# Half of an expert's down product as three float32r products, and two expert weights stored in 4 KB rows

## The chip, the cores and the metric

The kernel runs on one core of a Trainium2 chip. The metric is the device time of one execution in microseconds (us). A core has five engines that run side by side and meet through semaphores: TensorE (PE in the profile; its weight loads are listed apart as PEld), VectorE (DVE), ScalarE (ACT), GpSimd (POOL) and SyncE (SP, which here only issues transfers). Each engine works through its own instructions in program order.

## The reference

One encoder layer over 1,024 prompt tokens and 256 sample tokens of width 1,024, all in float32: a modulated RMS norm, an input projection, two token mixers (neighbourhood attention and multi-head latent attention), a gated merge, an output projection, and a mixture of experts; then a last norm. Only the mixture of experts is touched. A router gives each of the 1,280 tokens one of 4 groups and in it 2 of 8 experts, so 2,560 pairs of a token and an expert go to 32 experts. For each block of up to 128 tokens of one expert:

```
def expert_block(args):
    xb, e = args
    return (jax.nn.silu(xb @ w1[e]) * (xb @ w3[e])) @ w2[e]
```

with `w1[e]` and `w3[e]` of 1024 x 512 and `w2[e]` of 512 x 1024. The result is weighted and added to the token's row.

## The kernel before

The kernel goes through the layer in stages. The last long one is the expert stage, from about 1195 us to 1812 us: one block of 128 rows for each of the 32 experts, written out as a Python loop over `e` from 0 to 32, and after it a loop on the chip for experts with more than 128 tokens. With these inputs that loop runs zero times: the trace has 32 blocks.

A TensorE product takes a stationary operand (128 x 128) and a moving operand (128 rows, up to 512 columns). Two kinds of product occur here. A product of two float32 operands is recorded by the trace as two matrix instructions. The other kind is float32r, a reduced form, recorded as one. To keep the accuracy of float32 with it, the kernel splits a float32 array into a high part (the array rounded to float32r) and a low part (what is left), and adds up three products: high by high, low by high, high by low. `w_split` does this for a weight tile of 128 x 1024: ScalarE writes the high part (line 1399), VectorE subtracts it for the low part (line 1400).

An expert's weights come as 12 tiles of 512 KB ("quarters"): four of W1 (`m` is 0), four of W3 (`m` is 1), four of W2 (`m` is 2). `w_load` (line 1394) issues each on SyncE's queue into a free slot of 4 KB in each partition. A quarter of W1 or W3 is two blocks of 128 x 512, so that a partition receives two rows of 2 KB; a quarter of W2 is one block of 128 x 1024, one row of 4 KB. `w_ahead` issues the next loads of the fixed order `stream` as soon as slots are free, so loads run far ahead of use. Splits run three quarters ahead: when quarter i is taken (`w_next`), `w_fill` puts the split of quarter i + 3 into the programs of ScalarE and VectorE. The parts lie in a ring of 8 slots, four pairs, so the split of quarter i + 3 waits until TensorE is done with quarter i - 1.

The order of the work in a pass of the loop over `e`, the same on every engine:

- `up(0)` for expert e (line 1540): 24 float32r products, 4 quarters of 6; then ScalarE's silu (line 1545)
- `aT` for expert e - 1: 4 transposes of the activations on TensorE (line 1553), a copy of the 128 x 512 result by ScalarE (line 1555)
- `up(1)` for expert e: again 24 products; then VectorE's product with the silu (line 1547)
- `xT` for expert e + 1: 8 transposes of its gathered rows (line 1527), split by ScalarE (line 1529) and VectorE (line 1530); its rows come from `gather` (line 1370), issued by GpSimd
- `down` for expert e - 1: first the row `y` of gains (lines 1560 and 1561), then for each of 4 quarters of W2 two float32 products, one for each half of the 1,024 columns (line 1566), then VectorE's two scalings (line 1571), and GpSimd's scatter that adds the rows to `x1_d` (line 1572)

`xH`, `xL` and `y` take their slots from a ring of three.

Of the kernel before, what the change touches and what calls it, by code (L numbers as in the profile page):

```python
# [10 lines left out]
F32 = mybir.dt.float32  # L11
F32R = mybir.dt.float32r
# [74 lines left out]
def f32(x):  # L87
    return x.bitcast(F32)


def v3(t, k):
    return t.rearrange("p (k n) -> p k n", k=k)
# [3 lines left out]
def kernel(ctx, tc, A, out_p, out_s, upto=99, dbg=None):  # L96
    nc = tc.nc
    ctx.enter_context(tc.manual_schedule())
    V, S, G, PE, SY = nc.vector, nc.scalar, nc.gpsimd, nc.tensor, nc.sync
# [974 lines left out]
    n = len(units)  # L1074
# [307 lines left out]

    W1, W3, W2 = [A[n][0] for n in ("expert_w1", "expert_w3", "expert_w2")]
    stream = [(e - (m == 2), m, q) for e in range(33) for m in range(3) for q in range(4) if 0 <= e - (m == 2) and (e < 32 or m == 2)]
    LEAD, ACTS = 3, 3

    def w_load(e, m, q):
        r = sl.get()  # L1390
        src = (W1, W3, W2)[m]
        src = src[e] if isinstance(e, int) else src[bass.ds(e, 1)].rearrange("o r n -> (o r) n")
        k = 2 if m < 2 else 1
        SY.dma_start(v3(r, k), src.rearrange("(k p) n -> p k n", p=128)[:, q * k:q * k + k, :])
        return r

    def w_split(r):
        hi, lo = sl.get(F32R, parts), sl.get(F32R, parts)
        S.copy(hi, r)  # L1399
        V.tensor_sub(lo, r, f32(hi))  # L1400
        sl.put(r)
        w_ahead(0)
        return hi, lo

    loaded, ready = {}, deque()
    halves = [k for k in stream if k[1] < 2]
    at = [0, 0, 0]

    def w_ahead(spare):
# [4 lines left out]

    def w_next(e, m, q):

        if m == 2:
            return loaded.pop((e, m, q))
        assert halves[at[2]] == (e, m, q)
        at[2] += 1  # L1420
        w_fill()
        return ready.popleft()
# [90 lines left out]
    class Block:  # L1513
# [36 lines left out]
        def aT(b):  # L1550
            p = psx.tile([128, 4, 128], F32, name="pt")
            for k in range(4):
                PE.transpose(p[:, k, :], b.a[:, k * 128:k * 128 + 128], ident)  # L1553
            b.aT_ = ep.tile([128, 4, 128], F32, name="aT")
            S.copy(b.aT_, p)  # L1555

        def down(b, quarter):

            y = sl.get(ring=acts)
            S.mul(y, g2[1], b.of[1])  # L1560
            V.scalar_tensor_tensor(y, g2[0], b.of[0], y, op0=OP.mult, op1=OP.add)
            ps = [psh.tile([128, 512], F32, name=f"py{hb}") for hb in range(2)]
            for k in range(4):
                w = quarter(2, k)
                for hb, p in enumerate(ps):
                    PE.matmul(p, b.aT_[:, k, :], w[:, hb * 512:hb * 512 + 512], start=(k == 0), stop=(k == 3))  # L1566
                sl.put(w)
                w_ahead(0)
            for hb, p in enumerate(ps):
                cs = slice(hb * 512, hb * 512 + 512)  # L1570
                V.scalar_tensor_tensor(y[:, cs], p, b.wcol, y[:, cs], op0=OP.mult, op1=OP.mult)  # L1571
            G.indirect_dma_start(out=x1_d, out_offset=bass.IndirectOffsetOnAxis(ap=b.ix, axis=0), in_=y,  # L1572
                                 in_offset=None, bounds_check=NTOK - 1, oob_is_err=False, compute_op=OP.add)
            sl.put(y)
# [50 lines left out]
    with tc.For_i(0, n_rv, 1):  # L1625
        pick = ep.tile([128, 4], F32, name="pick")
        V.tensor_scalar(c, left, -BIG, BIG, op0=OP.mult, op1=OP.add)
        V.tensor_add(c, c, io9)
        V.tensor_reduce(pick[:, 0:1], c, axis=AX.XY, op=OP.min)
        V.tensor_scalar(c, c, pick[:, 0:1], None, op0=OP.is_equal)  # L1630
        V.tensor_sub(left, left, c)
        for k in range(2):
            V.tensor_mul(c2[:, k], be[:, k], c)
            V.tensor_reduce(pick[:, 1 + k:2 + k], c2[:, k], axis=AX.XY, op=OP.add)
        eint = ep.tile([128, 1], I32, name="eint")
        V.tensor_copy(eint, pick[:, 2:3])
        posb = ep.tile([128, 2, NT], F32, name="posb")
        V.tensor_scalar(posb, pos, pick[:, 1:2], None, op0=OP.subtract)
        eq = ep.tile([128, 2, NT], F32, name="eq")
        V.tensor_scalar(eq, eid, pick[:, 2:3], None, op0=OP.is_equal)  # L1640
        R = ep.tile([128, 2, NT, 2], F32, name="oR")
        for k in range(2):
            V.tensor_mul(R[:, k, :, 0], eq[:, k], tok1)
            V.tensor_mul(R[:, k, :, 1], eq[:, k], wgt[:, k])
        ps = psx.tile([128, 4, 128], F32, name="pt")
        for k in range(2):
            for t in range(NT):
                oh = ep.tile([128, 128], F32, name="ooh", bufs=2)
                V.tensor_scalar(oh, iof, posb[:, k, t:t + 1], None, op0=OP.is_equal)
                PE.matmul(ps[:, 0, :2], oh, R[:, k, t, :], start=(k == 0 and t == 0), stop=(k == 1 and t == NT - 1))  # L1650
        osl = ep.tile([128, 5], F32, name="osl")
        V.tensor_copy(osl[:, 0:2], ps[:, 0, :2])
        V.tensor_scalar(osl[:, 2:3], osl[:, 0:1], 0.0, 4096.0, op0=OP.is_equal, op1=OP.mult)
        ix = ep.tile([128, 1], I32, name="oix")
        V.scalar_tensor_tensor(ix, osl[:, 0:1], -1.0, osl[:, 2:3], op0=OP.add, op1=OP.add)
        for g, op in enumerate((OP.is_le, OP.is_gt)):
            V.tensor_scalar(osl[:, 3 + g:4 + g], osl[:, 0:1], float(SP), None, op0=op)
        e_rv = SY.value_load(eint[0:1, 0:1], min_val=0, max_val=31)
        b = Block(ix, osl[:, 1:2], [osl[:, 3 + g:4 + g] for g in range(2)])
        b.gather()  # L1660
        raws = {(m, q): w_load(e_rv, m, q) for m in range(3) for q in range(4)}
        b.xT()
        quarter = lambda m, q: w_split(raws[m, q]) if m < 2 else raws[m, q]
        b.up(0, quarter)
        b.up(1, quarter)
        b.aT()
        b.down(quarter)
# [37 lines left out]
def layout(inputs):  # L1705

    a = {k: np.ascontiguousarray(inputs[k]) for k in _INS}
    q = a["w_uq"].reshape(1, 256, 8, 96)
    a["w_uq"] = np.ascontiguousarray(np.concatenate(
        [q[..., :64].reshape(1, 256, 512), q[..., 64:].reshape(1, 256, 256)], axis=2))  # L1710
    kv = a["w_ukv"].reshape(1, 128, 8, 128)
    a["w_ukv"] = np.ascontiguousarray(np.concatenate(
        [kv[..., :64].reshape(1, 128, 512), kv[..., 64:].reshape(1, 128, 512)], axis=2))
    inv = (np.float32(1.0) / np.power(np.float32(10000.0), np.arange(0, 32, 2, dtype=np.float32) / np.float32(32)))
    ang = np.arange(SP, dtype=np.float32)[:, None] * inv[None, :].astype(np.float32)
    c, s = np.cos(ang).astype(np.float32).T, np.sin(ang).astype(np.float32).T
    cs = np.stack([np.tile(np.concatenate(x), (4, 1)) for x in ((c, c), (-s, s))])
    a["rope_p"] = by_blocks(cs[..., None])[..., 0]
    a["rope_s"] = np.ascontiguousarray(cs[:, :, :SS])
    a["x_prompt"] = by_blocks(a["x_prompt"])  # L1720

    rpb = a.pop("na_rpb")[0]
    row, c8, col = np.arange(16), np.arange(8), np.arange(64)
    rs = np.clip(row - 4, 0, 8)
    rows = (row[None, :] >= rs[:, None]) & (row[None, :] < rs[:, None] + 8)
    dr = np.clip(row[None, :] - row[:, None] + 7, 0, 14)
    dc = 8 * (np.arange(3)[None, :, None] - 1) + c8[None, None, :] - c8[:, None, None]
    val = rpb[:, dr[:, None, None, :, None], np.clip(dc + 15, 0, 30)[None, :, :, None, :]]  # L1730
    m0 = np.broadcast_to(rows[:, None, None, :, None], val.shape[1:]) & (np.abs(dc) < 16)[None, :, :, None, :]
    m1 = m0 & ((dc >= -8) & (dc < 8))[None, :, :, None, :]
    a["nbias"] = np.ascontiguousarray(np.stack(
        [np.where(m, val, np.float32(NEG)).reshape(8, 128, 384) for m in (m0, m1)], axis=2).reshape(8, 128, 768))
    st = np.clip(col - 8, 0, 48)
    inside = (col[None, :] >= st[:, None]) & (col[None, :] < st[:, None] + 16)
    dr = np.arange(6)[None, :] + 5 - np.arange(2)[:, None]
    dc = np.clip(col[None, :] - col[:, None] + 15, 0, 30)
    val = rpb[:, dr[:, None, :, None], dc[None, :, None, :]]
    a["sbias"] = np.ascontiguousarray(np.where(inside[None, None, :, None, :], val, np.float32(NEG)).reshape(8, 128, 384))  # L1740
    return a
# [18 lines left out]
```

## Time and profile before

| | |
|---|---|
| time before, median of 3 runs | 1855.91 us (1853.6 to 1859.47) |
| the profiled execution's own time | 1854.83 us |
| its span, first to last instruction | 1853.1 us |
| TensorE busy | 1743.1 us, 94% of the span |
| VectorE busy | 1001.4 us, 54% |
| ScalarE busy | 838.8 us, 45% |
| expert weights loaded | 384 transfers of 512 KB |

In rows of the profile `out<-in` are the names of tiles (`s` is any slot, `ph` and `pt` and `py` are PSUM tiles), a count follows an x, and an arrow `<-` behind an idle time names what ended it. A busy share of an engine is an average over stages with different limits. The ends of matrix instructions are modelled, so a busy TensorE need not be at its peak.

### The profile page before, as it was taken

Reading aid. Unit: us, or ns where it says so; the run is one execution under the profiler, and the core shown is the slowest. Engines: PE = TensorE matmul, PEld = TensorE weight load, DVE = VectorE, ACT = ScalarE, POOL = GpSimd, SP = SyncE. Lnnn points to the kernel's source line nnn. Section 1 sums busy time; section 2 is a strip of 40 time slices with the busy share of each in tenths; the row PEclk is TensorE's granted clock in tenths of the full one; section 3 lists DMA queues with packets and bytes.
Section 4 is the critical chain, followed back from the end, with each engine's and each line's share of the span. In section 5 each row is a group of like instructions: output and inputs, shape, how many; then the busy total and the mean of one; then the engine's idle time right before and its main releaser. Section 6 shows DMA issues by size and latency. Waiting matters only on the chain.

```text
span 1853.1 us, 27078 instructions
## 1 busy us (share of the span) xinstructions
PE 1743.1 (94%) x9874; PEld 1357.6 (73%) x9874; DVE 1001.4 (54%) x1674; ACT 838.8 (45%) x1391; POOL 319.0 (17%) x329
## 2 busy tenths in 40 slices
PE   5999999999999999999899999699999999999991
PEld 4787777998888888767688877567676676766760
DVE  6324422111455655444357466777777777777764
ACT  6222222321455555666533213366556565655642
POOL 0010210000122222322333000111111111111110
PEclk9989999999999999999899999799999999999995
DMA  9335676536714442878977356899999999999916
GB/s 349 109 115 168 222 264 221 191 91 165 152 55 112 115 121 86 232 214 230 297 251 224 132 216 235 327 359 360 361 365 360 362 356 361 358 356 364 349 36 242
DMA packets 268848, 439.47 MB, mean 237 GB/s; under 512 B 31928, under 2 KB 131592, under 8 KB 268712
## 3 DMA queue, kind: packets, MB, share of 16 engines
q1 hardware_dynamic: 252008, 389.45, 62.8%
q0 software_dynamic: 13824, 37.77, 7.3%
q10 hardware_dynamic: 2880, 10.49, 1.4%
q8 instruction: 79, 1.29, 0.3%
q14 instruction: 57, 0.47, 0.1%
HBM read 367.53 MB, written 82.67 MB: 243 GB/s over the span
## 4 chain that ended last, share of the span: by engine, by line
PE 84%; DVE 5%; DMA 5%; issue 2%; ACT 2%; SPq 1%; POOL 1%; DVEq 0%; POOLq 0%; ACTq 0%; another core or an unknown queue 0%
PE ph L1540 19%; PE pg L432 13%; PE py L1566 11%; PE s L895 6%; PE pw L1303 5%; PE fp L766 5%; PE fp L678 4%; PE o L945 4%; PE tp L927 4%; PE pg L599 3%; PE pt L1527 2%; PE pg L341 1%; PE pg L557 1%; PE pt L1553 1%; DMA x_d<-s,idx 1%
## 5 line engine op out<-in xcount | busy, mean ns | idle before, releaser
L1540 PE MATMUL ph<-s,s 128*128 128x512 f32 x1536 | 377.0, 401 | 1.4 <-DVE s L1530 1.2
L1399 ACT CAST s<-s 128x1024 fp32r<-128x1024 f32 x256 | 265.9, 1055 | 194.2 <-PE ph L1540 193.9
L1540 PEld LDWEIGHTS ph<-s,s 128*128 128x128 f32 x1536 | 286.4, 188 | 73.8 <-issue 13.9
L1400 DVE TENSOR_TENSOR s<-s,s 128x1024 fp32r<-128x1024 f32 x256 | 304.5, 1221 | 63.7 <-ACT s L1399 57.4
L432 PE MATMUL pg<-s,s 128*128 128x512 f32 (+1 forms) x1416 | 270.2, 351 | 7.8 <-ACT s L182 4.2
L432 PEld LDWEIGHTS pg<-s,s 128*128 128x128 f32 x1416 | 226.8, 190 | 53.0 <-ACT s L182 4.9
L1566 PE MATMUL py<-s,aT 128*128 128x512 f32 x512 | 225.1, 592 | 0.7 <-ACT aT L1555 0.7
L917 POOL TENSOR_SCALAR s<-s,m 128x1024 f32<-128x1024 f32 (+2 forms) x160 | 122.8, 767 | 438.5 <-DVE m L916 363.6
L1566 PEld LDWEIGHTS py<-s,aT 128*128 128x128 f32 x512 | 94.8, 190 | 108.2 <-issue 100.0
L895 PE MATMUL s<-s,s 96*128 96x512 f32 (+2 forms) x592 | 147.7, 368 | 1.8 <-ACT s L913 1.4
L913 ACT ACTIVATE s<-s,m 128x1024 f32<-128x1024 f32 (+2 forms) x160 | 124.9, 781 | 46.6 <-DVE m L903 27.3
L929 ACT COPY s<-tp 128x512 f32<-128x512 f32 (+2 forms) x160 | 78.2, 488 | 120.5 <-PE tp L927 116.9
L895 PEld LDWEIGHTS s<-s,s 96*128 96x128 f32 (+1 forms) x592 | 109.9, 190 | 27.9 <-ACT s L913 2.3
L678 PE MATMUL fp<-s,s 128*128 128x512 f32 x384 | 126.4, 430 | 2.8 <-ACT s L682 2.6
L927 PE MATMUL tp<-ident,s 128*128 128x128 f32 x752 | 110.4, 275 | 9.8 <-POOL s L917 9.4
L183 DVE TENSOR_TENSOR s<-s,s 128x1024 fp32r<-128x1024 f32 x31 | 37.7, 1224 | 148.7 <-ACT s L182 137.0
L1303 PE MATMUL pw<-s,s 128*128 128x512 f32 x480 | 118.0, 400 | 0.0
L766 PE MATMUL fp<-s,s 128*128 128x512 f32 (+1 forms) x576 | 114.0, 359 | 2.8 <-DMA s<-ao_m 1.4
L903 DVE TENSOR_REDUCE m<-s 128x1 f32<-128x1024 f32 (+1 forms) x80 | 85.0, 1062 | 51.6 <-PE s L895 50.2
L1572 POOL DMA_INDIRECT x_d<-s,idx x32 | 71.7, 2242 | 231.1 <-DVE s L1571 116.1
L766 PEld LDWEIGHTS fp<-s,s 128*128 128x128 f32 x576 | 96.5, 191 | 20.1 <-DMA s<-ao_m 2.1
L927 PEld LDWEIGHTS tp<-ident,s 128*128 128x128 f32 x752 | 89.3, 141 | 25.3 <-POOL s L917 15.9
(225 smaller groups left out, 2012.3 us busy)
## 6 DMA issues: line engine op xcount, KB each, us to landing
s<-in_expert_w SPq DMA_DIRECT2D x384, 512.0 KB
s<-in_w_in SPq DMA_DIRECT2D x47, 512.0 KB
s<-in_ada_w POOLq DMA_DIRECT2D x32, 512.0 KB, 6.1
s<-nak_d SPq DMA_DIRECT2D x40, 256.0 KB
s<-in_x_prompt SPq DMA_DIRECT2D x16, 512.0 KB
s<-in_ada_w SPq DMA_DIRECT2D x16, 512.0 KB
s<-gate_d SPq DMA_DIRECT2D x16, 512.0 KB
gate_d<-s SPq DMA_DIRECT2D x16, 384.0 KB
```

What stands on the lines that cost most here:

```text
L432: PE.matmul(p[:m, :CHUNKS[c][1]], g.at(a, j, 0, m), b.at(j, c), start=(j == 0 and n == 0), stop=(j == KD - 1 and n == 2))
L678: PE.matmul(p, w.at(a, j), b.at(j, 0), start=(n == 0), stop=(n == 23))
L766: PE.matmul(p[:, :w], b.ws[i].at(u, x * 4 + j), o[:, v, :w], start=(m == 0), stop=(m == 11))
L895: PE.matmul(u.s[:, b, :u.w], a, c, start=(n == 0), stop=(n == len(ops) - 1))
L913: S.activation(u.out, u.src, AF.Exp, bias=u.m[:, 0:1], scale=u.sign, accum_out=u.m[:, 1:2])
L917: G.tensor_scalar(u.P[:, :u.n], u.P[:, :u.n], u.m[:, 2:3], 1.0, op0=OP.mult, op1=OP.mult)
L927: PE.transpose(tp[:w, i // 128, :], u.P[:, b * 512 + i:b * 512 + i + w], ident)
L1303: PE.matmul(b.p, x[b.c].at(k, b.c, b.k), w[:, k % 2, :], start=(k + i == 0), stop=(k == 7 and i == 2))
L1399: S.copy(hi, r)
L1400: V.tensor_sub(lo, r, f32(hi))
L1540: PE.matmul(p, a[:, 2 * q + k, :], v3(w, 2)[:, k, :], start=(q + k + i == 0), stop=(q == 3 and k == 1 and i == 2))
L1566: PE.matmul(p, b.aT_[:, k, :], w[:, hb * 512:hb * 512 + 512], start=(k == 0), stop=(k == 3))
```

## The change

Of the four quarters of W2, the first two are now split as W1 and W3 are, and their part of the down product is done in three float32r products each; the other two stay float32. So a pass splits 10 quarters instead of 8, and the order of the splits (`halves`) takes in the two quarters of W2 behind the eight of the expert that follows. In `aT` the first two of the four transposed blocks become a high part (ScalarE) and a low part (VectorE, straight from PSUM), and ScalarE copies the other two: one copy of 128 x 512 becomes three instructions of 128 x 256. The ring of parts keeps its 8 slots. On the host, W1 and W3 are stored in a new array `w13` such that each quarter's 4 KB for a partition lie in one row; the values and the slots' contents stay the same.

```
+    W13, W2 = A["w13"], A["expert_w2"][0].rearrange("e (q p) n -> e q p n", p=128)
+    def in_parts(m, q):
+        return m < 2 or q < 2
     def w_load(e, m, q):
         r = sl.get()
-        k = 2 if m < 2 else 1
-        SY.dma_start(v3(r, k), src.rearrange("(k p) n -> p k n", p=128)[:, q * k:q * k + k, :])
+        src = W13[:, m, q] if m < 2 else W2[:, q]
+        SY.dma_start(r, src[e] if isinstance(e, int) else src[bass.ds(e, 1)].rearrange("o p n -> (o p) n"))
...
-    halves = [k for k in stream if k[1] < 2]
+    halves = [k for k in stream if in_parts(*k[1:])]
...
-        if m == 2:
+        if not in_parts(m, q):
             return loaded.pop((e, m, q))
...
-            b.aT_ = ep.tile([128, 4, 128], F32, name="aT")
-            S.copy(b.aT_, p)
+            b.aH, b.aL = [ep.tile([128, 2, 128], F32R, name=n) for n in ("aH", "aL")]
+            S.copy(b.aH, p[:, :2])
+            V.tensor_sub(b.aL, p[:, :2], f32(b.aH))
+            b.aT_ = ep.tile([128, 2, 128], F32, name="aT")
+            S.copy(b.aT_, p[:, 2:])
...
-                    PE.matmul(p, b.aT_[:, k, :], w[:, hb * 512:hb * 512 + 512], start=(k == 0), stop=(k == 3))
-                sl.put(w)
+                    cs = slice(hb * 512, hb * 512 + 512)
+                    if k < 2:
+                        for i, (a, x) in enumerate(((b.aH, w[0]), (b.aL, w[0]), (b.aH, w[1]))):
+                            PE.matmul(p, a[:, k, :], x[:, cs], start=(k + i == 0), stop=False)
+                    else:
+                        PE.matmul(p, b.aT_[:, k - 2, :], w[:, cs], start=False, stop=(k == 3))
+                sl.put(*(w if k < 2 else (w,)))
...
+    a["w13"] = np.ascontiguousarray(np.stack([a.pop(n)[0] for n in ("expert_w1", "expert_w3")], axis=1)
+                                    .reshape(32, 2, 4, 2, 128, 512).swapaxes(3, 4)).reshape(32, 2, 4, 128, 1024)
```

## Rows read from the trace of the kernel before

**Rows 1.** Stretches: us, busy PE, PEld, DVE, ACT, POOL; clock, DMA share, GB/s.

```profile
1200.00:1220.00 20.00, 18.55 (x87) 15.03 (x86) 15.85 (x16) 16.15 (x19) 1.29 (x1) 1.00 1.02 381
1241.00:1260.15 19.15, 19.15 (x79) 13.27 (x78) 14.01 (x15) 11.29 (x13) 3.35 (x2) 1.00 1.01 364
1300.00:1700.00 400.00, 400.00 (x1586) 277.06 (x1585) 292.24 (x292) 235.77 (x271) 69.66 (x42) 1.00 1.01 360
1760.00:1800.00 40.00, 40.00 (x153) 27.03 (x152) 26.31 (x30) 19.11 (x22) 5.82 (x7) 1.00 0.19 42
```

**Rows 2.** The chain that ended last, in order of time: start, us, what.

```profile
1421.04 5.50 PE ph L1540 x24
1426.54 0.44 PE pt L1553 x4
1426.98 5.48 PE ph L1540 x24
1432.45 0.87 PE pt L1527 x8
1433.33 6.87 PE py L1566 x16
1440.20 5.50 PE ph L1540 x24
...
1796.58 6.88 PE py L1566 x16
1803.48 0.76 DVE s L1571
```

**Rows 3.** The costliest groups of the page: count, busy us, mean ns, idle before.

```profile
L1540 PE MATMUL ph<-s,s 128*128 128x512 f32 x1536 | 377.0, 401 | 1.4 <-DVE s L1530 1.2
L1566 PE MATMUL py<-s,aT 128*128 128x512 f32 x512 | 225.1, 592 | 0.7 <-ACT aT L1555 0.7
L1303 PE MATMUL pw<-s,s 128*128 128x512 f32 x480 | 118.0, 400 | 0.0
```

**Rows 4.** Groups by line and shape on ScalarE and VectorE.

```profile
L1399 ACT CAST s<-s 128x1024 fp32r<-128x1024 f32 x256 | 265.9, 1055 | 194.2 <-PE ph L1540 193.9 <-DMA s<-in_expert_w 0.3
L1555 ACT COPY aT<-pt 128x512 f32<-128x512 f32 x32 | 18.6, 580 | 10.2 <-PE pt L1553 10.2
L951 ACT CAST s<-o 128x256 fp32r<-128x256 f32 x40 | 14.5, 362 | 6.1 <-PE o L945 6.1
L1400 DVE TENSOR_TENSOR s<-s,s 128x1024 fp32r<-128x1024 f32 x256 | 304.5, 1221 | 63.7 <-ACT s L1399 57.4 <-DMA s<-in_expert_w 2.0
L400 DVE TENSOR_TENSOR s<-pg,s 128x256 fp32r<-128x256 f32 x8 | 3.3, 415 | 0.0
```

**Rows 5.** VectorE in order of time, one pass: start, us, what, idle before it.

```profile
1439.38 1.61 DVE L1571 SCALAR_TENSOR_TENSOR s<-py,slots,s 128x512 f32<-128x512 f32 x2 [3.01 <-PE py L1566]
1440.90 1.22 DVE L1400 TENSOR_TENSOR s<-s,s 128x1024 fp32r<-128x1024 f32 x1
1442.48 1.23 DVE L1400 TENSOR_TENSOR s<-s,s 128x1024 fp32r<-128x1024 f32 x1 [0.36 <-ACT s L1399]
1443.86 2.58 DVE L1400 TENSOR_TENSOR s<-s,s 128x1024 fp32r<-128x1024 f32 x2 [0.16 <-ACT s L1399]
1447.78 4.63 DVE L1400 TENSOR_TENSOR s<-s,s 128x1024 fp32r<-128x1024 f32 x4 [1.34 <-ACT s L1399]
1454.23 1.28 DVE L1561 SCALAR_TENSOR_TENSOR s<-s,of,s 128x1024 f32<-128x1024 f32 x1
```

**Rows 6.** ScalarE in order of time, the same pass.

```profile
1452.08 1.07 ACT L1529 CAST s<-pt 128x512 fp32r<-128x512 f32 x2 [0.98 <-PE pt L1527]
```

**Rows 7.** Line 1394 from 1200 to 1800 us: its loads, first and last start.

```profile
L1394 SPq DMA_DIRECT2D s<-in_expert_w x345: 327/368/3076, 1200.1 to 1751.9; - x173
```

**Rows 8.** Line 1572 from 1240 to 1780 us: the scatters.

```profile
L1572 POOL DMA_INDIRECT x_d<-s,idx x28: 2300/2302/2307, 1249.7 to 1766.9; - x28
...
DMA to landing us min/median/max: 6.8/9.4/10.3
```

More of the change, by code (lines that the diff above doesn't have):

```diff
@@ L1381, in first_rows @@
         xg0.append(gather(idx[:, 0:1]))
-    W1, W3, W2 = [A[n][0] for n in ("expert_w1", "expert_w3", "expert_w2")]
+    W13, W2 = A["w13"], A["expert_w2"][0].rearrange("e (q p) n -> e q p n", p=128)
     stream = [(e - (m == 2), m, q) for e in range(33) for m in range(3) for q in range(4) if 0 <= e - (m == 2) and (e < 32 or m == 2)]
     LEAD, ACTS = 3, 3
+    def in_parts(m, q):
+        return m < 2 or q < 2
     def w_load(e, m, q):
         r = sl.get()
-        src = (W1, W3, W2)[m]
-        src = src[e] if isinstance(e, int) else src[bass.ds(e, 1)].rearrange("o r n -> (o r) n")
-        k = 2 if m < 2 else 1
-        SY.dma_start(v3(r, k), src.rearrange("(k p) n -> p k n", p=128)[:, q * k:q * k + k, :])
+        src = W13[:, m, q] if m < 2 else W2[:, q]
+        SY.dma_start(r, src[e] if isinstance(e, int) else src[bass.ds(e, 1)].rearrange("o p n -> (o p) n"))
         return r
@@ L1662 @@
         b.xT()
-        quarter = lambda m, q: w_split(raws[m, q]) if m < 2 else raws[m, q]
+        quarter = lambda m, q: w_split(raws[m, q]) if in_parts(m, q) else raws[m, q]
         b.up(0, quarter)
```

## The prediction

> **What bounds the kernel now.** I read the stretches first, to see which engine is full where the change acts. [...] A full TensorE row alone proves little, since the ends are modelled, and the DMA share is full as well. So I read the chain of waits next. In the stage it has no other engine and no transfer in it: 5.50 + 0.44 + 5.48 + 0.87 + 6.87 = 19.16 us, and the next pass begins where this one ended, 1421.04 to 1440.20 us [rows 2]. The same five pieces come back pass after pass. TensorE's own stream sets the pace, and the down product is 6.87 us of it.
>
> The DMA share looks like a second bound, so I asked what the loads wait for. The last of the expert weights is issued at 1751.9 us [rows 7], and from 1760 us the DMA share is 0.19 [rows 1], while TensorE only starts the last down product but one at 1796.58 us, with the last behind it [rows 2]. The loads end some 40 us, two passes, before their last use. They follow the slots that TensorE and VectorE give back; they do not hold TensorE up.
>
> **The change part by part.**
>
> *The products.* A float32 product is two records, so a pass has 16 records in 6.87 us: 0.429 us a record, 0.859 us a product. A float32r product of the same shape takes 5.48 / 24 = 0.2283 us in the second up product and 5.50 / 24 = 0.2292 us in the first [rows 2]. The change takes away four float32 products, 4 x 0.859 = 3.435 us, and puts twelve float32r products there, 12 x 0.2283 = 2.740 us. That is 0.695 us less in a pass. Over 32 passes it is 22.2 us; with 0.2292 us it is 21.9. The trace has no float32r product at line 1566. The slowest pace that float32r products of this shape show elsewhere is 118.0 / 480 = 0.246 us at line 1303 [rows 3]; with that a pass gains 0.485 us and the stage 15.5 us. I take 0.2283, because line 1540 is the same loop with the same kind of operands one instruction group away. A change of kind inside a product costs nothing that the chain shows: the up product behind the float32 one takes 5.50 us and the one behind transposes 5.48 [rows 2].
>
> [...]
>
> *Two more splits a pass.* ScalarE gets 2 x 1.055 us, VectorE 2 x 1.221 us [rows 4]. *The parts of the activations.* ScalarE's copy of 0.58 us becomes two of about 0.362 us, by the cast of the same 128 x 256 from PSUM; VectorE gets one more of 0.415 us, by the same subtraction from PSUM [rows 4]. ScalarE ends at 11.29 + 2.11 + 0.14 = 13.5 us, VectorE at 14.01 + 2.44 + 0.42 = 16.87 us, in a pass that I expect at 19.15 - 0.695 = 18.46 us. Both fit, VectorE with 1.6 us to spare. Fitting in sum isn't enough, since both work in order, so I place each piece. VectorE waits four times in a pass: 3.01 us before the scalings, then 0.36, 0.16 and 1.34 us before splits, 4.87 us in all [rows 5].
>
> - The order of the splits shifts by two. The run of four splits at 1447.78 us [rows 5] is now the last of W3, the two of W2 and the first of the next expert: still four, in the same place. The two that are pushed out come after the row `y` (it ends at 1454.23 + 1.28 us), where VectorE waits 3.01 us now. With the pass 0.695 us shorter that gap is 2.32 us against 2.44 us of splits, so the scalings start about 0.1 us later against TensorE.
> - The low part of the activations falls into the wait of 1.34 us before that run, and ScalarE's third instruction delays the run by 0.15 us.
> - So the split behind the scalings, needed by the fourth quarter of the next up product, comes about 0.3 us later. It ends now at 1440.90 + 1.22 = 1442.12 us; TensorE needs it at 1440.20 + 3 x 1.37 = 1444.3 us: 2.2 us of slack. The first of the run ends at 1449.0 us and is needed 5.50 + 0.44 + 4.1 us after 1440.20, at 1450.2: 1.2 us of slack. Both stay above zero, and the waits of 0.36, 0.16 and 1.34 us, of which 1.2 us remain, take up the delay within the pass.
>
> I therefore cost the splits at nothing on the path. What hides them is VectorE's idle time; without that cover each microsecond beyond it is lost in each pass.
>
> *W1 and W3 in 4 KB rows.* Off the path. With a pass of 18.46 us the stream must bring 364 x 19.15 / 18.46 = 378 GB/s to hold its lead [rows 1]. From 1200 to 1220 us, catching up, it brought 381 GB/s with rows of 2 KB [rows 1], so the rate exists. If it stayed at 360, the last load would still land at about 1760 us, and TensorE would reach its last products at about 1796.6 - 22 = 1774 us and after; the lead would shrink by about half and be enough. A gain outside this stage is possible only where TensorE waits at the beginning of the stage: it is idle 1.5 us from 1200 to 1220 us [rows 1], and that is all I allow for it. Below, I allow nothing: the quarters of W2 already come in one row of 4 KB.
>
> *Loads and slots.* The two quarters of W2 are read about three quarters earlier than now, some 5 us, out of a lead of 40, and their slots come free earlier. No queue gets an instruction more on SyncE or GpSimd. At the end, ScalarE's first copy before the last product is 0.2 us shorter and the low part may hold the second product by 0.3 us: nothing in sum.
>
> The sum against the profiled execution: 1854.83 - 22.2 = 1832.6 us. That execution lies 1.1 us below the median of the runs shown, well inside their spread.
>
> **The rivals.**
>
> *VectorE becomes the pace.* It holds if the three waits before splits (0.36 + 0.16 + 1.34 = 1.86 us) [rows 5] stay whole, because ScalarE's split waits for TensorE each time, and aren't eaten by work that comes late. Then a pass is 16.87 + 1.86 = 18.73 us, 0.42 us less than now, and the time 1854.83 - 13.4 = 1841.4 us. For it: VectorE goes from 73% to 91% of a pass. Against it: each of these waits is shown as waiting for ScalarE, and a VectorE that comes later finds ScalarE done.
>
> *Slower: the scatter holds the ring of three.* `y` goes back to the ring when its scatter has landed, and the next-but-one `xT` writes into that slot. The scatter of the pass shown starts right behind the scalings, at about 1441.2 us (1249.7 us and ten passes of 19.15 us), and lands 9.4 us later, 10.3 at most [rows 8], so at 1450.6 to 1451.5 us; ScalarE's write starts at 1452.08 us and waits for TensorE alone [rows 6]. The margin is 0.6 us at worst, and the scalings come later now. A late slot delays ScalarE and VectorE, whose splits have about 1.2 us to spare. It turns the gain into a loss when the landing slips by 0.6 + 1.2 + 0.7 = 2.5 us; at 3.1 us, the time would be 1854.83 + 32 x 0.6 = 1874 us. Against it: 28 scatters lie within 3.5 us of each other, and the slip I can derive is some 0.3 us.
>
> *The change doesn't do what it says.* If a float32r product took 0.286 us at line 1566, a third of a float32 one, the exchange would be even and the time 1855. Nothing in the rows comes near that: 0.246 us is the slowest.
>
> **How the numbers follow.** The forecast, 0.80: 1832.6 us, with a range of its own from 1828 (the 1.5 us at the start, and the runs' spread of some 3 us) to 1839.3 (0.246 us a product). VectorE as the pace, 0.09: 1841.4 us. No gain, 0.05: 1855 us. The scatter, 0.03: 1874 us. Something that I don't see, 0.03, taken as slower. The range reaches from 1828 to 1843 us, to take in VectorE's case with a little spread. About 0.3%, 5.6 us, is what can be told from no change: faster 0.89, same 0.05, slower 0.06.
>
> **What the profile after would show.** Right, if line 1566 has 12 + 8 records a pass and its piece of the chain falls from 6.87 to about 6.2 us, the pass to 18.46 us, TensorE stays without idle time, VectorE's busy time rises to about 16.9 us a pass, its wait before the scalings all but goes, and the DMA rate rises to about 375 GB/s. Wrong, if TensorE has waits for line 1400, if `aT`'s low part ends them, if the chain passes through VectorE or a scatter, or if float32r products there take over 0.24 us.

## The result, and the profile after

The change takes 1835.18 us (median of four executions, the profiled one among them) against 1855.32 us before (median of four; the table above has three of them), a ratio of 0.9886 with a 95% interval from 0.9861 to 0.9910. Forecast were 1833 us, in a range from 1828 to 1843. The profiled execution is not like the others: it took 1903.49 us, against 1831.44 to 1837.03 for the four without a profile, and the ratio is of the latter. So the profile below shows a case that the prediction knew only as a rival at 3 in 100, and the case that it forecast is shown by experiment 2.

The stretches of the profile after (columns as in [rows 1]) show both cases in one execution. Early, at 1241 us, TensorE is busy throughout and VectorE for 16.40 us of 18.46. From 1300 us on, TensorE is short of 30.6 us of 400:

```profile
1241.00:1259.46 18.46, 18.46 (x81) 13.95 (x81) 16.40 (x18) 13.15 (x16) 5.82 (x2) 1.00 1.02 392
1300.00:1700.00 400.00, 369.40 (x1505) 257.27 (x1503) 306.01 (x322) 244.17 (x303) 144.29 (x38) 1.00 0.90 326
```

The clock is 1.00 in both stretches, so it isn't the clock. The costliest groups of the page say which engine changed (line 1542 is now the up product, 1574 and 1576 the float32r and the float32 part of the down product, 1581 the scalings, 1582 the scatter, 1401 and 1402 the split's cast and subtraction, 1531 and 1532 `xH` and `xL`, 1558 the low part of the activations):

```profile
L1542 PE MATMUL ph<-s,s 128*128 128x512 f32 x1536 | 404.6, 409 | 42.5 <-DVE s L1402 35.2
L1402 DVE TENSOR_TENSOR s<-s,s 128x1024 fp32r<-128x1024 f32 x320 | 372.4, 1220 | 47.4 <-ACT s L1401 47.1
L1582 POOL DMA_INDIRECT x_d<-s,idx x32 | 166.0, 5188 | 303.4 <-DVE s L1581 280.2
...
L1576 PE MATMUL py<-s,aT 128*128 128x512 f32 x256 | 115.0, 592 | 0.0
L1531 ACT CAST s<-pt 128x512 fp32r<-128x512 f32 x64 | 34.5, 589 | 148.2 <-DMA x_d<-s,idx 125.5
```

GpSimd's scatter takes 5.19 us on average where each took 2.30 us [rows 8], and ScalarE waits 125.5 us in all for scatters to land, where it waited for TensorE alone [rows 6]. TensorE in turn waits 35.2 us for VectorE's low parts of the weights, the first of the prediction's signs of being wrong. In the chain that ended last (start, us, what) the TensorE pieces of [rows 2] are gone; a pass is one landing of 13.65 us, 7.1 us behind it in which the chain shows no wait ("issue") and a few short pieces, 21.04 us, until the last passes, where the down product shows as 2.81 + 3.43 us:

```profile
1439.22 13.65 DMA x_d<-s,idx
...
1452.91 7.11 issue
...
1460.26 13.55 DMA x_d<-s,idx
...
1810.27 2.81 PE py L1574 x12
1813.07 3.43 PE py L1576 x8
1816.51 5.49 PE ph L1542 x24
```

Where it begins is seen in three timelines of the same execution (start, us, what, idle before it). GpSimd's scatters, the first one of normal length:

```profile
1229.95 2.35 POOL L1582 DMA_INDIRECT x_d<-s,idx  x1 [6.01 <-DVE s L1581]
...
1249.08 4.58 POOL L1582 DMA_INDIRECT x_d<-s,idx  x1 [6.58 <-DMA s<-h_d,idx]
...
1268.41 5.71 POOL L1582 DMA_INDIRECT x_d<-s,idx  x1 [7.39 <-DVE s L1581]
```

ScalarE's `xH` in between, which waits for the landing of the first:

```profile
1241.76 1.07 ACT L1531 CAST s<-pt 128x512 fp32r<-128x512 f32 x2 [1.98 <-DMA x_d<-s,idx]
```

And VectorE behind the scalings, first with two short gaps, a pass later without:

```profile
1229.57 1.22 DVE L1402 TENSOR_TENSOR s<-s,s 128x1024 fp32r<-128x1024 f32 x1
1231.00 1.23 DVE L1402 TENSOR_TENSOR s<-s,s 128x1024 fp32r<-128x1024 f32 x1 [0.21 <-ACT s L1401]
1232.39 2.58 DVE L1402 TENSOR_TENSOR s<-s,s 128x1024 fp32r<-128x1024 f32 x2 [0.16 <-ACT s L1401]
...
1248.71 4.77 DVE L1402 TENSOR_TENSOR s<-s,s 128x1024 fp32r<-128x1024 f32 x4
1253.65 0.42 DVE L1558 TENSOR_TENSOR aL<-pt,aH 128x256 fp32r<-128x256 f32 x1 [0.17 <-ACT aH L1557]
```

VectorE's first gap (0.21 us, to 1231.00) opens 0.84 us behind the start of the first scatter, which ends at 1232.30 us. The second scatter starts while four splits run as one block and ends only at 1253.66 us, at the end of VectorE's next gap (0.17 us, to 1253.65). I read a loop in this: a scatter that lands late delays `xH`, then VectorE's splits; late splits find ScalarE done and run without gaps; without gaps GpSimd finishes its scatter late; the landing comes later still. Theory A is this loop, entered by a single late landing. Its rivals: that the loads in 4 KB rows crowd out the scatter's own transfer, or that VectorE simply has more work than a pass holds. The experiments had to tell these apart, and show what the change is worth without the loop.

### The profile page after: what moved, and what is told of

Read it like the earlier page. It is cut to its first block, busy times and chain, and to the rows that moved or that the text cites. A ratio compares the mean times of both kernels' runs of the same rounds, so it can differ in the third digit from the quotient of the medians.

```text
span 1901.8 us, 27748 instructions
## 1 busy us (share of the span) xinstructions
PE 1750.4 (92%) x10002; PEld 1371.8 (72%) x10002; DVE 1074.4 (56%) x1770; ACT 893.3 (47%) x1487; POOL 437.3 (23%) x329
## 4 chain that ended last, share of the span: by engine, by line
PE 53%; DMA 24%; issue 14%; DVE 5%; ACT 2%; POOL 1%; SPq 1%; POOLq 0%; DVEq 0%; ACTq 0%; another core or an unknown queue 0%
DMA x_d<-s,idx 19%; PE pg L432 12%; PE s L895 6%; PE pw L1303 5%; PE fp L766 5%; PE o L945 4%; PE fp L678 4%; PE tp L927 4%; PE pg L599 3%; PE ph L1542 2%; PE pg L341 1%; DMA s<-h_d,idx 1%; DMA s<-naq_d 1%; DMA s<-in_w_in 1%; PE pg L557 1%
## 5 line engine op out<-in xcount | busy, mean ns | idle before, releaser
L1542 PE MATMUL ph<-s,s 128*128 128x512 f32 x1536 | 404.6, 409 | 42.5 <-DVE s L1402 35.2
L1402 DVE TENSOR_TENSOR s<-s,s 128x1024 fp32r<-128x1024 f32 x320 | 372.4, 1220 | 47.4 <-ACT s L1401 47.1
L1542 PEld LDWEIGHTS ph<-s,s 128*128 128x128 f32 x1536 | 277.9, 188 | 151.8 <-DVE s L1402 70.1
L1401 ACT CAST s<-s 128x1024 fp32r<-128x1024 f32 x320 | 314.8, 1051 | 18.7 <-PE ph L1542 18.2
L1582 POOL DMA_INDIRECT x_d<-s,idx x32 | 166.0, 5188 | 303.4 <-DVE s L1581 280.2
L183 DVE TENSOR_TENSOR s<-s,s 128x1024 fp32r<-128x1024 f32 x31 | 37.7, 1224 | 149.5 <-ACT s L182 138.0
L1576 PE MATMUL py<-s,aT 128*128 128x512 f32 x256 | 115.0, 592 | 0.0
L1531 ACT CAST s<-pt 128x512 fp32r<-128x512 f32 x64 | 34.5, 589 | 148.2 <-DMA x_d<-s,idx 125.5
```

The source lines that it names most:

```text
L1542: PE.matmul(p, a[:, 2 * q + k, :], v3(w, 2)[:, k, :], start=(q + k + i == 0), stop=(q == 3 and k == 1 and i == 2))
```

## The experiments

**1. The same kernel again.** No edit.

> The changed kernel as it is. Its profiled execution took 1903.49 us, the four others 1831 to 1837. Theory A (GpSimd's scatter holds the ring of three, as in the rival): the 21.3 us pass of the profile is a loop that sustains itself, scatter 5.7 us on GpSimd, landing 13.6 us, ScalarE's xH cast behind it; an execution either falls into it (about 1900 us) or stays at TensorE's 18.46 us a pass (about 1833 us), so a new profile shows one of these two, and nothing between. Theory B (something outside the kernel slowed that one execution): the new profile shows 18.46 us a pass and scatters of 2.3 us on GpSimd that land after about 9.4 us.

Ratio 0.9885 (0.9861 to 0.9909). The four executions without a profile took 1830.36 to 1839.49 us, the profiled one 1903.68. Its scatters show the loop close up, one step a pass:

```profile
1228.41 2.35 POOL L1582 DMA_INDIRECT x_d<-s,idx  x1 [6.00 <-DVE s L1581]
...
1247.33 3.44 POOL L1582 DMA_INDIRECT x_d<-s,idx  x1 [6.35 <-DMA s<-h_d,idx]
...
1266.18 4.57 POOL L1582 DMA_INDIRECT x_d<-s,idx  x1 [6.68 <-DVE s L1581]
```

From 1300 us on all take 5.71 us. Both times came back, and no execution of this kernel lies between them.

**2. A ring of four** for `xH`, `xL` and `y`.

```
-    LEAD, ACTS = 3, 3
+    LEAD, ACTS = 3, 4
```

> The changed kernel with four slots instead of three in the ring of xH, xL and y, one slot less for loads. Theory A: xT no longer writes into the slot whose scatter is in flight, so ScalarE's cast at line 1531 waits for TensorE alone, the pass is 18.46 us in the profile too, 1831 to 1835 us, even though the scatter still takes about 5.7 us on GpSimd. Theory B: no difference from the changed kernel in the timed runs, and a profile that may be slow or not.

1832.14 us, ratio 0.9882 (0.9861 to 0.9903), the profiled execution among them (1831.42). That scatters would take 5.7 us even so was wrong: here they take 2.30 us. The chain, in order of time, is the one forecast:

```profile
1463.56 3.43 PE py L1576 x8
1466.99 5.49 PE ph L1542 x24
1472.48 0.44 PE pt L1555 x4
1472.92 5.48 PE ph L1542 x24
1478.39 0.87 PE pt L1529 x8
1479.27 2.81 PE py L1574 x12
1482.08 3.43 PE py L1576 x8
```

A pass is 18.52 us, the down product 6.24. The stretches of this kernel:

```profile
1241.00:1259.46 18.46, 18.46 (x82) 13.95 (x81) 16.39 (x18) 13.08 (x17) 3.54 (x2) 1.00 1.03 389
1300.00:1700.00 400.00, 400.00 (x1731) 303.28 (x1730) 354.34 (x367) 284.00 (x346) 76.45 (x43) 1.00 1.00 365
```

And VectorE in order of time behind the scalings of one pass:

```profile
1410.95 1.40 DVE L1581 SCALAR_TENSOR_TENSOR s<-py,slots,s 128x512 f32<-128x512 f32 x2
1412.28 1.21 DVE L1402 TENSOR_TENSOR s<-s,s 128x1024 fp32r<-128x1024 f32 x1
1413.70 1.23 DVE L1402 TENSOR_TENSOR s<-s,s 128x1024 fp32r<-128x1024 f32 x1 [0.22 <-ACT s L1401]
1415.09 2.58 DVE L1402 TENSOR_TENSOR s<-s,s 128x1024 fp32r<-128x1024 f32 x2 [0.16 <-ACT s L1401]
```

The wait of 3.01 us before the scalings [rows 5] is gone, as forecast; the gap of 0.22 us is what GpSimd lives on: the scatter beside these lines runs from 1412.64 to 1414.95 us, so that gap opens 0.85 us behind its start and 1.46 us before its end. That it ends in the second gap, of 0.16 us, is no more than a coincidence: in the trace of before a scatter of 2.30 us has the gap of 0.36 us [rows 5] at the same place and is over 0.1 us before the one of 0.16 us opens.

**3 and 4. One half of the change alone.** In 3 only the 4 KB rows (`in_parts` is `m < 2`, `aT` and the down product as before); in 4 only the products, from rows of 2 KB.

```
 3:      def in_parts(m, q):
-        return m < 2 or q < 2
+        return m < 2
 4:  -    W13, W2 = A["w13"], ...
     +    W1, W3, W2 = [A[n][0] for n in ("expert_w1", "expert_w3", "expert_w2")]
```

> The down product as before, in float32; only W1 and W3 in rows of 4 KB. If the loads are off the path, as the prediction has it: 1855 us within 0.3%, pass 19.15 us, the DMA share below the 1.00 of before. If the loads held TensorE up somewhere: up to 1.5 us less, or more if the stage before gains as well.

> The three products in half of the down product; W1 and W3 in rows of 2 KB as before. If the lead of the loads covers the faster pass, as the prediction has it: the same as the changed kernel, 1832 to 1836 us, with a DMA rate of 361 to 378 GB/s. If 4 KB rows are needed to keep up: the pass stays near 19.15 us once the lead is used up, 1845 to 1855 us. The ring of three can hold this kernel as it can the changed one.

The rows alone: 0.9997 (0.9982 to 1.0012), no change. The products alone: 1834.91 us, 0.9889 (0.9864 to 0.9914), the whole gain. The stretch from 1300 to 1700 us moved 355 GB/s with the products alone and 365 in experiment 2; TensorE was busy for 400 us of 400 in both. Experiment 4 keeps the ring of three, and its profiled execution (1834.40 us) came close to the loop and out again. ScalarE's `xH` in it (its lines are two further on), two passes:

```profile
1241.15 1.07 ACT L1533 CAST s<-pt 128x512 fp32r<-128x512 f32 x2 [0.94 <-DMA x_d<-s,idx]
...
1259.56 1.08 ACT L1533 CAST s<-pt 128x512 fp32r<-128x512 f32 x2 [0.83 <-PE pt L1531]
```

The first scatter of the stage landed 10.7 us after its start here, 11.7 in the profile after, 11.5 in experiment 1; in the trace of before that one and the next lie at 9.2 to 10.1 us. A wait for it of 0.94 us still left VectorE its gaps; waits of 1.76 us (experiment 1) and 1.98 us didn't. The late first landing is no accident of two executions: it is 11.5 us in experiment 2 and 11.4 in experiment 9 below too, which have both halves of the change and other rings, and there no loop follows. With the 4 KB rows alone it is 9.8. So the late landing goes with both halves together, as far as one trace each without the one or the other can say, and the ring decides whether a loop comes of it. What makes that landing late stays open.

**5 and 6. More VectorE work where the gaps are:** a subtraction of 128 x 512 (0.68 us) behind the scalings, with a ring of four (5) and of three (6). For its room the pool has 48 slots, not 49.

```
-NSLOT = 49
+NSLOT = 48
...
+            V.tensor_sub(ep.tile([128, 512], F32, name="more"), g2[0][:, :512], g2[1][:, :512])
```

> Ring of four and, behind the two scalings of each pass, one more subtraction of 128 x 512 on VectorE into a tile that nobody reads (about 0.69 us), so that VectorE's splits after it run without the short gaps; one slot less for loads. Theory A (VectorE without gaps holds GpSimd's scatter, and the ring of three turns that into lost time): the scatter at line 1583 takes about 5.7 us on GpSimd and lands after about 14 us in every pass, and the time stays at 1832 us within 0.3%, pass 18.5 us, since with four slots nobody waits for it. Theory C (the scatter was slow because the pass was slow, not the other way round): the scatter stays at 2.3 us.

> The same added subtraction with the ring of three. Theory A: every execution now falls into the loop, profiled or not: ScalarE's cast in xT waits for the scatter in every pass, pass about 21.5 us, 1900 to 1915 us. Theory C or a cause outside the kernel: about 1835 us in the timed runs, as the added 0.69 us fit into VectorE's idle time.

1922.03 us (1.0366, from 1.0349 to 1.0383) and 1943.80 us (1.0477, from 1.0445 to 1.0508), in every execution, with a profile or without; 6 is above the 1900 to 1915 us expected. The scatter from 1300 to 1700 us (now line 1583; min/median/max in ns, first and last start) and the wait for it (us in total, times, longest), of 5 and then of 6:

```profile
L1583 POOL DMA_INDIRECT x_d<-s,idx x19: 6309/6313/6315, 1311.0 to 1689.2; - x19
...
DVE s L1532 <- DMA x_d<-s,idx: 37.6, 13, 4.2
```

```profile
L1583 POOL DMA_INDIRECT x_d<-s,idx x18: 6307/6312/6316, 1313.1 to 1687.3; - x18
...
ACT s L1531 <- DMA x_d<-s,idx: 85.7, 16, 6.3
```

So one part of theory A stands: filled gaps stretch the scatter, now to 6.31 us, its landing to 14.8, and a pass to 378.2 / 18 = 21.0 us (5) and 374.2 / 17 = 22.0 us (6). The other part fell: a ring of four isn't immune. It moves the wait from ScalarE's `xH` to VectorE's `xL`, which then takes the slot that `y` gives back. Experiment 2 was free because its scatters stayed at 2.3 us.

**7 and 8. Three and four quarters of W2 in products, ring of four, 48 slots.**

```
 7:  -        return m < 2 or q < 2
     +        return m < 2 or q < 3
 8:  +        return True
```

> Three quarters of W2 split instead of two, ring of four, one slot less for loads. TensorE's pass falls by another two exchanges, 2 x 0.174 = 0.347 us, to 18.17 us; VectorE's work rises to 16.39 + 1.22 + 0.13 = 17.74 us. If VectorE's remaining waits (the 1.39 us behind the low part of the activations above all) leave room: 1832 - 11 = 1821 us. If VectorE becomes the pace: pass 17.74 plus 1.0 to 1.6 us of waits, 18.7 to 19.3 us, 1840 to 1858 us.

> All four quarters split, ring of four, one slot less for loads. TensorE alone would need 17.82 us a pass; VectorE's work is 16.39 + 2.44 + 0.26 = 19.1 us. VectorE as the pace: at least 19.1 us a pass, with its wait of 1.4 us 20.5 us, so 1851 to 1896 us and waits of TensorE for the splits. If instead TensorE stayed the pace: about 1810 us.

1925.43 us (1.0390, from 1.0373 to 1.0408) and 1961.07 us (1.0580, from 1.0559 to 1.0600). Scatters of 5.71 us in both, with waits of `xL` for them of 43.8 and 56.1 us in 400, and passes of 378.3 / 18 = 21.0 and 378.5 / 17 = 22.3 us. Both times are above everything expected. More products in float32r bring more splits, and the loop takes back more than they give. In 8 TensorE also waits for splits in the down product, 56.8 us of 400, so it is no clean test of the loop.

**9. `y` in a ring of its own.** `xH` and `xL` share two slots, `y` has two others, so no cast waits for a landing of the pass before.

```
-    LEAD, ACTS = 3, 3
+    LEAD, ACTS = 3, 2
...
-            y = sl.get(ring=acts)
+            y = sl.get(ring=ys)
...
+    parts, acts, ys = sl.ring(2 * LEAD + 2), sl.ring(ACTS), sl.ring(2)
```

> The changed kernel with a ring of two slots of its own for y, and a ring of two for xH and xL: now no write of xT can land in a slot whose scatter is in flight, neither ScalarE's of xH nor VectorE's of xL (with the ring of four the next xL took y's slot). Theory A: 1832 us, profiled or not, pass 18.52 us, no wait for a scatter on any engine. If the wait only moves once more: some engine shows waits for x_d and some executions lie near 1900 us.

1833.54 us, 0.9890 (0.9874 to 0.9907), passes of 18.52 us. All executions lie within 1832.63 to 1834.08, the profiled one too. In the stage no cast waits for a scatter to land, and TensorE is full. The 4 KB rows don't crowd out the scatters' transfers beyond the first: at 365 GB/s they land after 9.8 us in the middle (9.4 before):

```profile
1300.00:1700.00 400.00, 400.00 (x1726) 302.10 (x1725) 354.61 (x367) 282.45 (x345) 76.34 (x43) 1.00 1.00 365
```

**10. As 9, with the subtraction of 5** and 48 slots. **11. As 9, with three quarters**, 48 slots, and `aT`'s copy ahead of its low part.

> The same rings with the added subtraction of 128 x 512 behind the scalings, which made the ring of three 1944 us and the ring of four 1922 us. Theory A: the scatter takes 6.3 us on GpSimd and lands after about 14.8 us as in those runs, but nobody waits for it: 18.5 to 18.7 us a pass, 1832 to 1838 us. If the added 0.69 us themselves made those two runs slow (VectorE as the pace), they do it here too: 1900 us or more.

> Three quarters of W2 split, the rings of e9, and ScalarE's copy of the last activation block put ahead of VectorE's low part. TensorE alone: 18.17 us a pass. VectorE: 17.5 us of work as in the run with three quarters before, plus its wait behind the low part, 1.39 us there and less here. If the scatter alone held that run at 21.1 us a pass: 18.2 to 18.9 us, 1822 to 1845 us. If VectorE's work holds it: nearer 21.

Inside the stage both do what the loop's removal promises. The scatters of 10 and 11 from 1300 to 1700 us, and the stretch itself in 11:

```profile
L1583 POOL DMA_INDIRECT x_d<-s,idx x22: 4042/4609/5180, 1301.4 to 1690.3; - x22
```

```profile
L1582 POOL DMA_INDIRECT x_d<-s,idx x22: 5707/5710/5712, 1301.8 to 1683.9; - x22
```

```profile
1300.00:1700.00 400.00, 400.00 (x1804) 316.27 (x1803) 384.69 (x397) 310.97 (x374) 148.43 (x44) 1.00 1.00 365
```

They are long, though in 10 shorter than the 6.3 us expected; nobody on the path waits for them, TensorE is busy for 400 us of 400 in both, and a pass is 18.52 us (10) and 18.19 us (11). Yet the times are 1852.70 us (0.9997, from 0.9986 to 1.0008) and 1842.54 us (0.9942, from 0.9925 to 0.9960), 19 us above what these passes give. The loss lies ahead of the stage. Its first transposes on TensorE in 9 and in 11:

```profile
1193.39 1.97 PE L1529 MATMUL pt<-ident,s 128*128 128x128 f32 x8 [2.29 <-DMA s<-h_d,idx]
```

```profile
1209.73 1.97 PE L1529 MATMUL pt<-ident,s 128*128 128x128 f32 x8 [2.02 <-DMA s<-h_d,idx]
```

16.3 us later, and from 1209.08 to 1213.09 in the other runs with 48 slots (5 to 8 and 10), where all those with 49 lie from 1189.5 to 1193.6, the kernel before among them. Before this I had put the whole time of 5 and 6 down to the loop; some 20 us of each belong to the missing slot, as they do in 7 and 8.

**12. As 11, with 49 slots.** The room comes from a tile of the loop that runs zero times.

```
-NSLOT = 48
+NSLOT = 49
...
-                oh = ep.tile([128, 128], F32, name="ooh", bufs=2)
+                oh = ep.tile([128, 128], F32, name="ooh", bufs=1)
```

> Three quarters of the down product in float32r products with a ring of two for y, as e11, but with 49 slots as the kernel before has: the room is taken from a tile that the kernel's last loop would use twice over and that no pass of this input touches. Theory A (the some 20 us that e10 and e11 lost outside the stage are the price of one slot less in the stages before: the first transpose of the experts' stage came at 1209.73 us in e11 and at 1193.39 in e9): the first transpose comes at about 1193.4 again, a pass stays 18.19 us as in e11, and the time is that of e9 less 32 passes x (18.52 - 18.19) = 10.6, about 1823 (1820 to 1827). Rival B (the loss belongs to the third quarter, whose splits and extra VectorE work disturb something before or behind the steady passes): the first transpose still comes after 1205, or a pass is longer than 18.4, and the time stays at 1838 to 1846. Rival C (with 49 slots the third quarter's scatters of 5.7 us hold someone again): a wait for the scatter's landing of over 1 us a pass on ScalarE or VectorE, and over 1850.

1823.81 us (1822.47 to 1826.91), 0.9835 (0.9817 to 0.9852): some 10 us under experiment 9. The first transposes, the chain of a pass, and the scatter with its landing:

```profile
1191.39 1.97 PE L1529 MATMUL pt<-ident,s 128*128 128x128 f32 x8 [2.27 <-DMA s<-h_d,idx]
```

```profile
1451.76 5.48 PE ph L1542 x24
1457.23 0.87 PE pt L1529 x8
1458.11 4.21 PE py L1574 x18
1462.32 1.72 PE py L1576 x4
1464.04 5.47 PE ph L1542 x24
```

```profile
L1582 POOL DMA_INDIRECT x_d<-s,idx x22: 5707/5710/5716, 1302.4 to 1684.5; - x22
...
DMA to landing us min/median/max: 13.1/13.3/14.2
```

Here the scatter takes 5.71 us and lands after 13.3, much as in the profile after, and costs nothing, because no cast waits for it. Theory A of this run held; a slot less costs some 18 us before the stage (1209.73 against 1191.39 us).

## Why the prediction was right, and where it wasn't

- *The products*: right. Twelve float32r products take 2.81 us against the forecast 2.740, eight float32 records 3.43, so the piece falls from 6.87 to 6.24 us (forecast about 6.2) and the pass to 18.52 (18.46). One product is 2.81 / 12 = 0.234 us, above 0.2283, within the bound of 0.246. Experiment 12's 4.21 / 18 gives 0.234 too, so it goes with each product and is no fixed price of a change of kind; why it is more than at line 1542 stays open. The bound was read amiss: by the same measure, busy time of the page, line 1540 itself has 377.0 / 1536 = 0.245 us, so line 1303 showed no slower pace. The gain is 0.63 us a pass, 20.2 us in the stage, where I had 22.2.
- *The splits hidden in VectorE's idle time*: right where the loop doesn't run. VectorE is busy for 16.4 us a pass (forecast 16.87; back-to-back instructions overlap a little: above, the split at 1412.28 us starts before the scalings end at 1412.35), the scalings follow a split without a wait, and TensorE has no idle time from 1300 to 1700 us. The rival of VectorE as the pace didn't come, nor did it at 17.5 us a pass in experiment 11 (384.69 us busy in 400, TensorE full).
- *4 KB rows off the path*: right in time (experiments 3 and 4). The rate rose to 365 GB/s rather than 375. The lead shrank and was enough: the last load of a weight starts 28.2 us before the last down product but one in experiment 2 (1746.7 and 1774.9 us), against 44.7 before; with rows of 2 KB, in experiment 4, 14.0 us are left (1763.8 and 1777.8).
- *The scatter holding the ring of three*: this rival I sized wrongly, in chance and price. The step was "the slip I can derive is some 0.3 us", with the turn into a loss at 2.5 us. It took the scatter's 2.30 us on GpSimd for a constant and added up VectorE's waits as room to be used up. They weren't free room: the 0.2 us gap behind the first split is what lets GpSimd get on. With the ring of three one landing of 11.5 to 11.7 us instead of 9.4 (10.1 for the same scatter before) closes it, and the loop holds the pass at about 21 us and the time at 1903, not 1874. My 28 scatters within 3.5 us of each other came from a VectorE with gaps, and left out the first scatter of the stage. (The slot goes to the next `xT` behind the scatter, as the rows used there have it, not to the next but one.)
- *Products no cheaper*: didn't come.

The forecast held for every execution without a profile. The two with a profile of this kernel both fell into the loop, and none of eight without. That those eight stayed out was luck as far as the prediction goes: its margin for the landing was 0.6 us beyond a worst landing of 10.3, and in all four traces with both halves the first landing of the stage took 11.4 us or more. Whether the profile makes that landing late stays open, since an execution without one leaves no trace; experiment 4's profiled execution stayed out.

## What to carry to other kernels

Before filling an engine's idle gaps, ask which neighbour lives on them: here a gap of 0.2 us in VectorE's work decided how long GpSimd's scatter took. A buffer whose slot returns only with a transfer's landing should not share a ring with the operands of the next pass; separating them cost no time (1833.54 us against 1832.14 with the ring of four) and let a third quarter pay (1823.81). Compare stages, not only totals: a slot taken for an experiment cost 18 us ahead of the place under study, some 14 of them 900 us ahead (line 570's first product starts at 277.8 us in experiment 12 and at 292.0 in 11).

## What the hardware showed unexpectedly

GpSimd's indirect scatter of the same 128 rows took 2.30 us where a gap of 0.21 to 0.36 us in VectorE's work opened 0.85 us behind its start, and 3.44, 4.57, 5.71 and 6.31 us as that gap closed. From the opening of the first gap of 0.2 us or more to the scatter's end it was 1.4 to 1.5 us in the trace of before and in experiments 2, 4, 9, 11 and 12, and 1.1 us in the loop of the profile after, where that gap is one of 1.39 us. VectorE's subtractions kept their 1.22 us meanwhile.

The instructions beside which the scatter grew from 2.30 to 6.31 us are float32 subtractions, most of them of two SBUF tensors. Why filled gaps hold it is not shown: which access of the scatter waits, and for what, no run here shows.
